# Activation tiles at a wider stride, one chain for keys and values, and shorter norms in an encoder block

## The chip, the core and the metric

The kernel runs on one core of one Trainium2 chip. The time is device microseconds from the start of the program to its end; several executions are taken and their median is given.

## The reference, cut to what matters

One block of an encoder on 256 positions and 2,048 channels, with 256 memory positions, all in float32:

```python
mem_n = rms_norm(mem, mem_norm_g)
h = rms_norm(x, norm_g[0])
q, k, v, g, lr, u_f, u_h, u_s = split(h @ w_in)
y_a = gla_mixer(q, k, v, g, lr, ...)                       # gated linear attention, two directions
y_b = rms_norm(fnet_mixer(u_f), grp_norm_g[0])             # Fourier mixing
y_c = rms_norm(hyena_mixer(u_h, ...), grp_norm_g[1])       # long convolutions
y_d = rms_norm(shortconv_mixer(u_s, sc_conv_w), grp_norm_g[2])
x = x + concatenate([y_a, y_b, y_c, y_d]) @ w_out
x = x + cross_attention(rms_norm(x, norm_g[1]), mem_n, w_xq, w_xkv, w_xo)   # 4 heads of 512
x = x + swiglu(rms_norm(x, norm_g[2]), w_gate_up, w_down)  # 5,632 hidden channels
return rms_norm(x, final_norm_g)
```

`rms_norm(x, g)` is `x * rsqrt(mean(x*x) + 1e-6) * g` over the channels. The group norms `y_b`, `y_c`, `y_d` go over 512 channels each, `y_a` is normed inside its mixer.

## The kernel before

**Tiles.** Activations are kept transposed: 128 channels on the partitions, 256 positions along a partition. A matrix product has to be exact to float32, so each activation tile is `[128, 512]` words: columns 0 to 255 hold the value rounded to the matmul's format (`hi`), 256 to 511 the rest (`lo`). Each 128x128 weight block is likewise split into `wh` and `wl`. One block of a product then takes two matmuls (`mm`, lines 273 and 274): `wh` against all 512 columns, and `wl` against the 256 columns of `hi`. The text calls this a wide block. The two halves of the result are added later by `merge` (line 280, a copy on ScalarE, and an addition on VectorE through the helper at line 178). A narrow block (lines 270, 271, 274) puts all three products in the same 256 columns. 24 tiles `act0` to `act23` lie one behind the other in each partition and serve every stage; the attention adds four `oex` and two `pt` tiles and slots for keys and values, the last stage 36 `f` tiles.

**Weights.** The weights come as one stream `W` in the order of use, in slabs of 128 x 2,048 words (1 MB), issued by SyncE (line 79). A half slab is split by ScalarE (line 89) and VectorE (line 90) ahead of its use. While the list `st.after` has entries, each transfer of a weight piece is followed on the same queue by the next entry; at the start these entries are the loads of the 16 tiles of `mem`.

**Order of the work.** TensorE runs the matrix products in the order `w_xkv`, `w_in`, `w_out`, `w_xq`, `w_xo`, `w_gate_up`, `w_down`. Everything else (mixers, norms, loads of keys and values, softmax) is written as generators in a `Background` queue. After each block, `mm` calls `poll`, which lets a generator take a step when its planned time has come and when VectorE isn't planned to be behind; `drain` runs one generator, or all, to the end. A generator that yields `SOON` (0.01 us) may go on at once, otherwise after 1.3 us (`LAG`). The framework then schedules the instructions for each engine and adds the waits; each engine runs its own queue in order.

**Norms.** `rstd_begin` sums squares over the partitions with matmuls against a column of ones (line 215), one for each half of the positions and for each tile that it is given, and `rstd_cols` takes the inverse root in a few operations on two columns (lines 226 to 237): by an integer first guess and three Newton steps, or, with `root=True` (the final norm alone), by ScalarE's square root, a reciprocal and one step. `rstd_bank` spreads the result over all partitions with two diagonal tiles (line 248) and a matmul (line 250). `group_norm` (lines 499 to 515) squares four tiles on ScalarE and gives all four to `rstd_begin`; three of the four groups are normed by it.

**Keys and values.** `w_xkv` writes keys and values to DRAM in pieces of 128 KB. `load_kv(hd)` brings one head's eight pieces back into tiles `mr` (six buffers, issued by GpSimd, line 576) and splits them (lines 186, 194 and 178); the generators of two heads can be under way together. Before a head's scores are queued, its loads are drained.

**End.** The last `w_down` column is added to the residual, squared and summed; the residual tiles are multiplied by the norm on VectorE (six pairs) and GpSimd (two pairs, line 697), and SyncE stores each pair (256 KB, line 700).

Of the kernel before, what the change touches and what calls it, by code (L numbers as in the profile page):

```python
# [13 lines left out]
F32 = mybir.dt.float32  # L14
# [93 lines left out]
class Background:  # L108
# [32 lines left out]
    def drain(self, g=None):  # L141
        while True:
            q = [e for e in self.q if g is None or e[0] is g]
            if not q:
                break
            for e in q:
                self.step(e)


class Block:  # L150
# [54 lines left out]
    def rstd_begin(self, accs, n, keep=None, root=False):  # L205
# [11 lines left out]
        return self.rstd_cols(p[:, 0:m], n, keep, root)  # L217

    def rstd_cols(self, p, n, keep=None, root=False):
# [7 lines left out]
        if root:  # L227
            nc.scalar.activation(a, v, AF.Sqrt)
            nc.vector.reciprocal(y, a)
# [105 lines left out]
    def run(self):  # L335
        nc, cp = self.nc, self.cp
        st = self.st
        self.act = [cp.tile([P, 512], F32R, name=f"act{i}") for i in range(24)]
# [20 lines left out]
        st.after = [lambda a=a: load("memT", *a) for a in ((1, 1), (2, 1), (3, 1), (4, 1), (5, 1), (6, 2), (8, 2), (10, 2), (12, 2), (14, 2))]  # L359
# [139 lines left out]
    def group_norm(self, y, grp, slots, wait=None):  # L499
# [3 lines left out]
        yield  # L503
        yield
        col = self.rstd_begin([sq], 512)
# [42 lines left out]
    def attention(self):  # L548
        tc, nc, act, st = self.tc, self.nc, self.act, self.st
        with tc.tile_pool(name="atp", bufs=1) as atp, tc.tile_pool(name="kp", bufs=1) as kp, \  # L550
                tc.tile_pool(name="mp", bufs=6) as mp:
# [5 lines left out]
            kv = [None] * 4  # L557
# [11 lines left out]
            def load_kv(hd):  # L569

                kt, vh, vl = [], [], []
                ms = []
                for src in (self.kd, self.vd):
                    for i in range(4 * hd, 4 * hd + 4):
                        ms.append(mp.tile([P, R], F32, name="mr", tag="mr"))
                        nc.gpsimd.dma_start(ms[-1], src[:, i * R:(i + 1) * R])
# [637 lines left out]
```

## Time and profile before

| | us |
|---|---|
| median of 3 runs | 1532.26 |
| lowest to highest | 1532.22 to 1533.97 |
| the profiled execution, its own time | 1531.54 |
| its span in the trace | 1529.7 |
| TensorE busy | 1507.0 |
| TensorE weight loads busy | 1315.1 |
| VectorE busy | 990.7 |
| ScalarE busy | 787.2 |

The span runs from the first to the last recorded instruction, so the profiled execution's own time is 1.8 us longer. Busy times come from the span; weight loads (PEld) overlap the matmuls. The mean granted clock of TensorE was 0.995 of full speed. In the rows that follow, a timeline row gives the start in us, the duration in us, engine, source line, operation, the tiles (output, then inputs) and how many instructions it holds, and in brackets how long the engine had been idle and what ended that. A row of groups gives the count, the busy time in us and the mean in ns. A row of stretches gives the stretch, its length, and for PE and PEld the busy time and the number of instructions, then the granted clock, the DMA engines' busy share and their GB/s. A row of waits gives the total in us, the number of waits and the longest.

### The profile page before, as it was taken

What the parts mean: (1) busy time and instruction counts of PE and PEld (TensorE: products, weight loads), DVE (VectorE), ACT (ScalarE), POOL (GpSimd) and SP (SyncE); (2) the same over time, 40 slices, a digit from 0 to 9 for tenths busy, and PEclk for the clock granted to TensorE, in tenths of its full rate; (3) what the DMA queues carried; (4) which work ended last, traced back from release to release, by engine and by line L of the source; (5) the groups of instructions that cost most, each with busy time, mean ns of one, the idle gap of its engine ahead of it and who ended that gap; (6) DMA issues with size and microseconds to landing.
All of it is one profiled execution on the core that took longest, in us unless ns stands there. A gap on an engine that the chain in (4) does not pass through costs nothing.

```text
span 1529.7 us, 22321 instructions
## 1 busy us (share of the span) xinstructions
PE 1507.0 (99%) x8830; PEld 1315.1 (86%) x8830; DVE 990.7 (65%) x1525; ACT 787.2 (51%) x1238; POOL 39.9 (3%) x76
## 2 busy tenths in 40 slices
PE   8999999999999899999999999999999999999996
PEld 7877788889999788888888888888888888888886
DVE  6676668678656767767766666666666664545553
ACT  6664455547445656656555444444444444444442
POOL 0100100000001100000000000000000000000000
PEclk9999999999999999999999999999999999999998
DMA  9865554354346655444545555555555555555552
GB/s 352 342 237 191 198 190 165 138 190 172 127 167 203 227 187 190 159 151 154 190 169 190 192 193 193 193 189 186 187 186 192 190 192 193 188 179 185 192 193 83
DMA packets 48664, 290.53 MB, mean 190 GB/s; under 512 B 6157, under 2 KB 7470, under 8 KB 16816
## 3 DMA queue, kind: packets, MB, share of 16 engines
q1 hardware_dynamic: 45344, 280.64, 51.7%
q0 software_dynamic: 3072, 8.39, 1.5%
q8 instruction: 69, 1.13, 0.3%
q14 instruction: 35, 0.29, 0.1%
q10 hardware_dynamic: 144, 0.08, 0.0%
HBM read 282.80 MB, written 6.29 MB: 189 GB/s over the span
## 4 chain that ended last, share of the span: by engine, by line
PE 96%; DMA 2%; DVE 1%; ACT 0%; issue 0%; SPq 0%; POOL 0%; DVEq 0%; POOLq 0%; ACTq 0%
PE pg L273 49%; PE pg L274 27%; PE pg L270 3%; PE pg L271 3%; PE pg L325 3%; PE pg L327 2%; PE pg L326 2%; PE pm L273 1%; PE pm L770 1%; DMA mr<-values 1%; PE pm L215 1%; PE pm L620 1%; PE pm L647 0%; PE pm L274 0%; DMA mr<-keys 0%; PE pm L250 0%
## 5 line engine op out<-in xcount | busy, mean ns | idle before, releaser
L273 PE MATMUL pg<-act,wh 128*128 128x512 f32 x2680 | 940.0, 394 | 9.3 <-DVE tmp L178 4.7
L90 DVE TENSOR_TENSOR wl<-raw,wh 128x1024 fp32r<-128x1024 f32 (+1 forms) x507 | 616.9, 1218 | 429.4 <-ACT wh L89 426.0
L274 PE MATMUL pg<-act,wl 128*128 128x256 f32 x3008 | 842.2, 281 | 0.0
L89 ACT CAST wh<-raw 128x1024 fp32r<-128x1024 f32 (+1 forms) x507 | 529.7, 1046 | 592.5 <-PE pg L273 337.4
L273 PEld LDWEIGHTS pg<-act,wh 128*128 128x128 f32 x2680 | 504.5, 188 | 122.7 <-DVE tmp L178 5.1
L274 PEld LDWEIGHTS pg<-act,wl 128*128 128x128 f32 x3008 | 566.9, 189 | 2.6 <-issue 1.6
L273 PE MATMUL pg<-f,wh 128*128 128x512 f32 x540 | 191.3, 399 | 0.0
L274 PE MATMUL pg<-f,wl 128*128 128x256 f32 x576 | 161.8, 281 | 0.0
L273 PEld LDWEIGHTS pg<-f,wh 128*128 128x128 f32 x540 | 101.5, 188 | 25.2
L274 PEld LDWEIGHTS pg<-f,wl 128*128 128x128 f32 x576 | 108.8, 189 | 0.0
L270 PE MATMUL pg<-act,wh 128*128 128x256 f32 x328 | 94.7, 289 | 0.0
L271 PE MATMUL pg<-act,wh 128*128 128x256 f32 x328 | 92.1, 281 | 0.0
L178 DVE TENSOR_TENSOR tmp<-pg,tmp 128x256 f32<-128x256 f32 x183 | 76.1, 417 | 5.0 <-ACT tmp L280 4.0
L280 ACT COPY tmp<-pg 128x256 f32<-128x256 f32 x179 | 64.8, 363 | 14.3 <-PE pg L274 14.3
L325 PE MATMUL pg<-wh,act 128*128 128x512 f32 x160 | 66.4, 415 | 0.0
L327 PE MATMUL pg<-wh,act 128*128 128x512 f32 x160 | 63.3, 396 | 0.0
L326 PE MATMUL pg<-wl,act 128*128 128x512 f32 x160 | 62.9, 393 | 0.0
L270 PEld LDWEIGHTS pg<-act,wh 128*128 128x128 f32 x328 | 61.9, 189 | 0.7
L271 PEld LDWEIGHTS pg<-act,wh 128*128 128x128 f32 x328 | 61.9, 189 | 0.3
L178 DVE TENSOR_TENSOR tmp<-tmp,rs 128x256 f32<-128x256 f32 x88 | 37.3, 425 | 2.9
L325 PEld LDWEIGHTS pg<-wh,act 128*128 128x128 f32 x160 | 30.0, 188 | 10.4 <-issue 2.9
L326 PEld LDWEIGHTS pg<-wl,act 128*128 128x128 f32 x160 | 30.1, 188 | 7.5 <-issue 1.0
(227 smaller groups left out, 985.9 us busy)
## 6 DMA issues: line engine op xcount, KB each, us to landing
raw<-in_W SPq DMA_DIRECT2D x248, 1024.0 KB, 4.8
res<-in_xT SPq DMA_DIRECT2D x8, 512.0 KB, 4.9
raw<-in_W SPq DMA_DIRECT2D x7, 512.0 KB, 7.8
k<-in_mem SPq DMA_DIRECT2D x8, 256.0 KB, 7.7
k<-in_x SPq DMA_DIRECT2D x8, 256.0 KB, 8.3
keys<-tmp POOLq DMA_DIRECT2D x16, 128.0 KB, 5.5
values<-tmp POOLq DMA_DIRECT2D x16, 128.0 KB, 2.3
mr<-keys POOLq DMA_DIRECT2D x16, 128.0 KB, 3.5
```

The costliest lines, as they stand in the source:

```text
L89: nc.scalar.copy(wh[:, a:b], r[:, a:b])
L90: nc.vector.tensor_tensor(out=wl[:, a:b], in0=r[:, a:b], in1=wh[:, a:b].bitcast(F32), op=ALU.subtract)
L178: self.nc.vector.tensor_tensor(out=out, in0=a, in1=b, op=op)
L215: nc.tensor.matmul(p[:, 2 * g + r:2 * g + r + 1], a[:, r * P:(r + 1) * P], self.ones[:, 0:1], start=i == 0, stop=i == len(acc) - 1)
L270: self.nc.tensor.matmul(p[:, 0:R], wh, slot[:, 0:R], start=start, stop=False)
L271: self.nc.tensor.matmul(p[:, 0:R], wh, slot[:, R:512], start=False, stop=False)
L273: self.nc.tensor.matmul(p[:, :], wh, slot[:, :], start=start, stop=False)
L274: self.nc.tensor.matmul(p[:, 0:R], wl, slot[:, 0:R], start=False, stop=stop)
L280: self.nc.scalar.copy(t, p[:, R:512])
L325: nc.tensor.matmul(ps[r][:, :], hi, wh, start=k == 0, stop=False)
L326: nc.tensor.matmul(ps[r][:, :], hi, wl, start=False, stop=False)
L327: nc.tensor.matmul(ps[r][:, :], lo, wh, start=False, stop=k == nk - 1)
```

## The change

Six edits.

- Each `act` tile is 520 words wide, of which the first 512 are used: the tiles lie 2,080 bytes apart in a partition instead of 2,048, and all that is laid out behind them moves by 768 bytes. The buffers `mr` go from six to five.
- The list `st.after` begins with two entries that do nothing, so that the loads of `mem` after the first come two weight pieces later on the queue.
- `group_norm` adds its four squares on VectorE and gives `rstd_begin` the one sum.
- One generator `load_kv` fetches and splits all four heads' keys and values in one chain; a head's scores are a generator that waits for its keys and values, and at the start of the products of heads 2 and 3 the scores of the head two before are drained, other generators being stepped along with it.
- The final norm adds the squares up over the partitions and spreads the sums in one matmul against a full tile of ones, and takes the root on 256 columns. `root` goes out of the helpers.
- The stores alternate between SyncE's queue and ScalarE's.

```diff
--- before.py
+++ after.py
@@ -138,12 +138,12 @@
             if self.owed < OWED and self.now >= e[1]:
                 self.step(e)
 
-    def drain(self, g=None):
+    def drain(self, g=None, others=False):
         while True:
             q = [e for e in self.q if g is None or e[0] is g]
             if not q:
                 break
-            for e in q:
+            for e in list(self.q) if others else q:
                 self.step(e)
 
 
...
@@ -224,15 +224,11 @@
         c = keep.tile([P, 24], F32, name=f"krc{next(self.kept)}") if keep else self.rp.tile([P, 24], F32, name="rc", tag="rc")
         y, v, a = (c[:, 8 * i:8 * i + m] for i in range(3))
         nc.vector.tensor_scalar(out=v, in0=p, scalar1=1.0 / n, scalar2=EPS, op0=ALU.mult, op1=ALU.add)
-        if root:
-            nc.scalar.activation(a, v, AF.Sqrt)
-            nc.vector.reciprocal(y, a)
-        else:
-
-            nc.vector.tensor_scalar(out=a.bitcast(U32), in0=v.bitcast(U32), scalar1=1, scalar2=None, op0=ALU.logical_shift_right)
-            nc.vector.tensor_scalar(out=y.bitcast(I32), in0=a.bitcast(I32), scalar1=-1.0, scalar2=float(0x5f3759df),
-                                    op0=ALU.mult, op1=ALU.add)
-        for _ in range(1 if root else 3):
+
+        nc.vector.tensor_scalar(out=a.bitcast(U32), in0=v.bitcast(U32), scalar1=1, scalar2=None, op0=ALU.logical_shift_right)
+        nc.vector.tensor_scalar(out=y.bitcast(I32), in0=a.bitcast(I32), scalar1=-1.0, scalar2=float(0x5f3759df),
+                                op0=ALU.mult, op1=ALU.add)
+        for _ in range(3):
             self.stt(a, y, -0.5, y, ALU.mult, ALU.mult)
             self.tt(a, a, v, ALU.mult)
             self.stt(y, a, 1.5, y, ALU.add, ALU.mult)
@@ -335,7 +331,7 @@
     def run(self):
         nc, cp = self.nc, self.cp
         st = self.st
-        self.act = [cp.tile([P, 512], F32R, name=f"act{i}") for i in range(24)]
+        self.act = [cp.tile([P, 520], F32R, name=f"act{i}")[:, 0:512] for i in range(24)]
         self.res = [cp.tile([P, 4, R], F32, name=f"res{i}") for i in range(4)]
         self.resk = lambda i: self.res[i // 4][:, i % 4, :]
         self.vec = cp.tile([P, NV], F32, name="vec")
@@ -356,7 +352,8 @@
         nc.vector.memset(warm, 1.0)
         nc.scalar.copy(warm, warm)
         load("memT", 0, 1)
-        st.after = [lambda a=a: load("memT", *a) for a in ((1, 1), (2, 1), (3, 1), (4, 1), (5, 1), (6, 2), (8, 2), (10, 2), (12, 2), (14, 2))]
+        st.after = [lambda: None, lambda: None]
+        st.after += [lambda a=a: load("memT", *a) for a in ((1, 1), (2, 1), (3, 1), (4, 1), (5, 1), (6, 2), (8, 2), (10, 2), (12, 2), (14, 2))]
         nc.vector.memset(self.ones, 1.0)
         make_identity(nc, self.ident)
         with self.tc.tile_pool(name="wx", bufs=1) as st.extra:
@@ -501,8 +498,10 @@
         for j in range(4):
             self.nc.scalar.activation(sq[j], y[:, j, :], AF.Square)
         yield
-        yield
-        col = self.rstd_begin([sq], 512)
+        for j in range(3):
+            self.tt(sq[j + 1], sq[j], sq[j + 1], ALU.add)
+        yield
+        col = self.rstd_begin([sq[3:]], 512)
         yield
         yield
         rs = self.rstd_end(col)
@@ -548,13 +547,13 @@
     def attention(self):
         tc, nc, act, st = self.tc, self.nc, self.act, self.st
         with tc.tile_pool(name="atp", bufs=1) as atp, tc.tile_pool(name="kp", bufs=1) as kp, \
-                tc.tile_pool(name="mp", bufs=6) as mp:
+                tc.tile_pool(name="mp", bufs=5) as mp:
             oex = [atp.tile([P, 512], F32R, name=f"oex{i}") for i in range(4)]
             pt = [atp.tile([P, 512], F32R, name=f"pt{i}") for i in range(2)]
             qs = atp.tile([P, 2], F32, name="qs")
             o = act[0:8] + oex + act[8:12]
             slot = lambda name, n: kp.tile([P, 512], F32R, name=name, tag=name, bufs=n)
-            kv = [None] * 4
+            kv = [([], [], []) for _ in range(4)]
 
             def ev_q(q, p):
                 q.append(slot("q", 8))
@@ -566,39 +565,57 @@
                 nc.vector.tensor_scalar(out=qs, in0=col, scalar1=512 ** -0.5, scalar2=None, op0=ALU.mult)
                 yield
 
-            def load_kv(hd):
-
-                kt, vh, vl = [], [], []
-                ms = []
-                for src in (self.kd, self.vd):
-                    for i in range(4 * hd, 4 * hd + 4):
-                        ms.append(mp.tile([P, R], F32, name="mr", tag="mr"))
-                        nc.gpsimd.dma_start(ms[-1], src[:, i * R:(i + 1) * R])
+            heads = []
+
+            def load_kv():
+
+                todo = [(hd, what, i) for hd in range(4) for what in range(2) for i in range(4)]
+                parts = []
+
+                def fetch():
+                    if len(parts) < len(todo):
+                        hd, what, i = todo[len(parts)]
+                        m = mp.tile([P, R], F32, name="mr", tag="mr")
+                        o = (4 * hd + i) * R
+                        nc.gpsimd.dma_start(m, (self.vd if what else self.kd)[:, o:o + R])
+                        parts.append(m)
+
+                for _ in range(5):
+                    fetch()
+                yield 4
+                for n, (hd, what, i) in enumerate(todo):
+                    while hd > len(heads) + 1:
+                        yield
+                    if what == 0:
+                        kv[hd][0].append(slot("kt", 8))
+                        self.split(kv[hd][0][-1], parts[n])
+                    else:
+                        if i % 2 == 0:
+                            kv[hd][1].append(slot("vh", 4))
+                            kv[hd][2].append(slot("vl", 4))
+                        c = slice(i % 2 * R, i % 2 * R + R)
+                        self.split2(kv[hd][1][-1][:, c], kv[hd][2][-1][:, c], parts[n])
+                    fetch()
+                    yield 1.0
+
+            def scores(hd, q):
+                while len(kv[hd][2]) < 2:
+                    yield
                 yield
-                for m in ms[:4]:
-                    kt.append(slot("kt", 8))
-                    self.split(kt[-1], m)
-                    yield SOON
-                for i, m in enumerate(ms[4:]):
-                    if i % 2 == 0:
-                        vh.append(slot("vh", 4))
-                        vl.append(slot("vl", 4))
-                    c = slice(i % 2 * R, i % 2 * R + R)
-                    self.split2(vh[-1][:, c], vl[-1][:, c], m)
-                    yield SOON
-                kv[hd] = kt, vh, vl
+                yield from self.head(q, *kv[hd], pt, o[4 * hd:4 * hd + 4], qs)
+                heads.append(hd)
 
             lp = [list(range(8)), list(range(8, 16))]
             self.bg.add(scales())
-            loads = [self.bg.add(load_kv(0))]
+            self.bg.add(load_kv())
+            gens = []
             for hd in range(4):
-                if hd < 3:
-                    loads.append(self.bg.add(load_kv(hd + 1)))
                 q = []
+                if hd > 1:
+                    self.bg.drain(gens[hd - 2], True)
                 self.gemm("w_xq", [(4 * hd + i) * P for i in range(4)], self.h2, lambda i, p: ev_q(q, p), first=(4, lp),
                           before=lambda n: n and hd == 0 and self.bg.drain(self.late))
-                self.bg.drain(loads[hd])
-                self.bg.add(self.head(q, *kv[hd], pt, o[4 * hd:4 * hd + 4], qs))
+                gens.append(self.bg.add(scores(hd, q)))
             h3 = self.h3 = act[12:24] + act[0:4]
 
             def ev_o(i, p):
@@ -688,8 +705,17 @@
 
             self.gemm("w_down", [i * P for i in range(16)], f, ev_down,
                       first=(4, [list(range(40)), list(range(40, 44))]), narrow_last=True)
-            p = self.rstd_bank(self.rstd_begin([[self.acc, last]], D, root=True))
-            rs = self.tmp()
+
+            p = self.bank()[:, 0:R]
+            for i, a in enumerate((self.acc, last)):
+                nc.tensor.matmul(p, self.ones, a, start=i == 0, stop=i == 1)
+            v, y, a, rs = (self.tmp() for _ in range(4))
+            nc.vector.tensor_scalar(out=v, in0=p, scalar1=1.0 / D, scalar2=EPS, op0=ALU.mult, op1=ALU.add)
+            nc.scalar.activation(a, v, AF.Sqrt)
+            nc.vector.reciprocal(y, a)
+            self.stt(a, y, -0.5, y, ALU.mult, ALU.mult)
+            self.tt(a, a, v, ALU.mult)
+            self.stt(p, a, 1.5, y, ALU.add, ALU.mult)
             nc.scalar.copy(rs, p)
             for i in range(0, KT, 2):
                 x = self.res[i // 4][:, i % 4:i % 4 + 2, :]
@@ -697,7 +723,7 @@
                     nc.gpsimd.tensor_tensor(out=x, in0=x, in1=rs.unsqueeze(1).to_broadcast([P, 2, R]), op=ALU.mult)
                 else:
                     self.tt(x, x, p.unsqueeze(1).to_broadcast([P, 2, R]), ALU.mult)
-                nc.sync.dma_start(self.t["out"][:, i * R:(i + 2) * R], x.rearrange("p k r -> p (k r)"))
+                (nc.scalar if i % 4 else nc.sync).dma_start(self.t["out"][:, i * R:(i + 2) * R], x.rearrange("p k r -> p (k r)"))
 
 
 class Hyena:
```

More of the change, by code (lines that the diff above doesn't have):

```diff
@@ L203, in sumsq, with rstd_begin @@
             self.tt(acc, acc, s, ALU.add)
-    def rstd_begin(self, accs, n, keep=None, root=False):
+    def rstd_begin(self, accs, n, keep=None):
         nc = self.nc
@@ L216, in rstd_begin, with rstd_cols @@
                                      start=i == 0, stop=i == len(acc) - 1)
-        return self.rstd_cols(p[:, 0:m], n, keep, root)
-    def rstd_cols(self, p, n, keep=None, root=False):
+        return self.rstd_cols(p[:, 0:m], n, keep)
+    def rstd_cols(self, p, n, keep=None):
         nc = self.nc
```

## The prediction

> **What bounds the kernel now.** I read the page first: busy time per engine, the chain that ended last, the costliest groups.
>
> ```profile
> PE 1507.0 (99%) x8830; PEld 1315.1 (86%) x8830; DVE 990.7 (65%) x1525; ACT 787.2 (51%) x1238; POOL 39.9 (3%) x76
> PE 96%; DMA 2%; DVE 1%; ACT 0%; issue 0%; SPq 0%; POOL 0%; DVEq 0%; POOLq 0%; ACTq 0%
> L273 PE MATMUL pg<-act,wh 128*128 128x512 f32 x2680 | 940.0, 394 | 9.3 <-DVE tmp L178 4.7
> L273 PE MATMUL pg<-f,wh 128*128 128x512 f32 x540 | 191.3, 399 | 0.0
> ```
>
> TensorE is busy for 99% of the span and 96% of the chain runs over it. So there are three ways to change the time: fewer matmuls, a different pace of the same matmuls, or the few gaps. The gaps stand in the waits of PE:
>
> ```profile
> PE pg L273 <- DVE tmp L178: 4.7, 1, 4.7
> PE pg L273 <- DVE act L182: 4.6, 1, 4.6
> PE pm L250 <- DVE dg L248: 1.8, 1, 1.8
> PE pm L273 <- ACT wh L89: 1.0, 1, 1.0
> ```
>
> One is the first load, one the last norm (L250), one a wait for weights soon after the start, and one, of 4.7 us, lies in mid-run. For the pace I asked for the busy time of three stretches, each from the start of one "wide block" (a 512-column matmul L273 with its 256-column L274) to the start of another:
>
> ```profile
> 801.75:807.29 5.54, 5.54 (x17) 3.00 (x17) 1.00 0.54 189
> 722.51:728.10 5.59, 5.59 (x17) 3.00 (x17) 1.00 0.54 188
> 1329.63:1345.11 15.48, 15.48 (x46) 8.27 (x45) 1.00 0.57 204
> ```
>
> The first holds 16 blocks on act tiles: 346.5 ns each. The second is a w_xo column, 12 blocks on act tiles and 4 on oex tiles. The third is a w_down group of 8 blocks on act and 36 on f tiles: 44 x 0.3465 would be 15.25.
>
> **Part 1, the stride.** The act tiles' width goes from 512 to 520 words, so tile k moves by 32k bytes. Act tiles sat on multiples of 64 bytes; now every odd one sits 32 bytes past one. oex, pt and f tiles sit 32 bytes past one already, so they show what an "off" tile costs. It isn't nothing: (15.48 - 15.25) / 36 = 6 ns a block in the third stretch, (5.59 - 5.54) / 4 = 12 in the second, where the rounding of the ends leaves 10 to 15 and I use 10. But an off tile in w_down follows other off tiles; after the change each odd tile follows an even one. The starts inside the second stretch, and a stretch where off blocks of the background mix in:
>
> ```profile
> 725.29 0.40 PE L273 MATMUL pg<-oex,wh 128*128 128x512 f32 x1
> 725.98 0.40 PE L273 MATMUL pg<-oex,wh 128*128 128x512 f32 x1
> 726.69 0.40 PE L273 MATMUL pg<-act,wh 128*128 128x512 f32 x1
> 727.40 0.39 PE L273 MATMUL pg<-act,wh 128*128 128x512 f32 x1
> ...
> 693.20 0.40 PE L273 MATMUL pg<-oex,wh 128*128 128x512 f32 x1
> 695.99 0.39 PE L273 MATMUL pg<-act,wh 128*128 128x512 f32 x1
> ```
>
> The first two off blocks after aligned ones take 0.69 together, what two aligned ones take; the next two take 0.71; then two aligned ones 0.71: part of the cost falls on later blocks. From 693.20 to 695.99 lie eight off blocks (4 on oex, 4 of L647 and L648 on pt; the rows between are left out): 0.349 each, 2 ns over. Half of the 2,680 wide blocks are on odd tiles, 1,340. The nearest rows to "one off block behind an aligned one" are the first pair (0 ns) and this mix (2 ns); I take 1.3 ns, **+1.8 us**. Ends: 0, and 10 ns for +13.4; the w_down price, 6, gives +8.0. Below nothing: the pair 725.29 to 725.98 is, by rounding, at best 2 ns a block under an aligned pair; no longer stretch is, so a gain is a rival and not the forecast.
>
> The Trainium skill bears on this: "SBUF — State Buffer", section "Door 1: The DMA port swizzle", has SBUF cachelines of 16 bytes, with a penalty when an access crosses into a new one. 2080 is 130 such lines, so by that rule an odd tile costs no more than an even one and this term would be 0; the f rows above do not agree with it for runs of off tiles, and the measurement decides.
>
> **Part 2, the group squares.** Each of three group norms sums four squares inside its column sums: 2 row halves x 4 tiles.
>
> ```profile
> 333.99 1.84 PE L215 MATMUL pm<-ones,tmp 128*128 128x1 f32 x16
> ...
> 458.11 1.84 PE L215 MATMUL pm<-ones,tmp 128*128 128x1 f32 x16
> ...
> 471.63 0.75 DVE L178 TENSOR_TENSOR act<-res,act 128x256 fp32r<-128x256 f32 x2
> 477.43 0.39 PE L273 MATMUL pg<-act,wh 128*128 128x512 f32 x1
> ```
>
> Sixteen records (two passes of each fp32 matmul) take 1.84; the first and the last of the three norms are shown. After, two matmuls, four records, are left: 12/16 x 1.84 x 3 = 4.1, of which I take **-4.0 us**, as the last record's overhang stays. It comes straight off a TensorE that waits for nothing there. Three adds of some 0.4 us (two of the same size: 0.75 in the fourth row) are put on VectorE, 65% busy, in each norm. Cover: the last norm's final splits end at 471.63 + 0.75 = 472.4 and w_out's first block, which reads them, starts at 477.43; 5 us cover 1.3 us of adds and a matmul or two of delay. Without that cover it would cost 1.3.
>
> **Part 3, the start.** Two weight pieces go to the queue ahead of two mem tiles.
>
> ```profile
> 4.60 1.19 PE L273 MATMUL pg<-act,wh 128*128 128x512 f32 x2 [4.60 <-DVE act L182]
> 8.54 1.21 PE L273 MATMUL pm<-act,wh 128*128 128x512 f32 x4 [1.05 <-ACT wh L89]
> 16.21 0.62 PE L273 MATMUL pg<-act,wh 128*128 128x512 f32 x2
> ```
>
> Between the first and the last row are 24 wide blocks: 11.61 against 24 x 0.3465 = 8.32, so 3.3 are lost, part to a half-rate clock on the first blocks, 1.05 to a named wait for weights. Weights that arrive 256 KB earlier take away most of that wait; mem tile 1 comes later but is needed only eight blocks in. **-0.9**, ends -1.5 (the wait and half of the rest) and +0.5 (a mem tile that comes late).
>
> **Part 4, keys and values.** The mid-run gap:
>
> ```profile
> 499.50 0.28 PE L274 MATMUL pg<-act,wl 128*128 128x256 f32 x1
> 504.52 0.80 PE L273 MATMUL pg<-act,wh 128*128 128x512 f32 x1 [4.74 <-DVE tmp L178]
> 509.81 0.41 PE L273 MATMUL pg<-act,wh 128*128 128x512 f32 x1
> ...
> 500.87 0.40 ACT L186 CAST kt<-mr 128x256 fp32r<-128x256 f32 x1 [3.35 <-DMA mr<-keys]
> 503.09 0.36 ACT L280 COPY tmp<-pg 128x256 f32<-128x256 f32 x1
> 504.05 0.42 DVE L178 TENSOR_TENSOR tmp<-pg,tmp 128x256 f32<-128x256 f32 x1
> ...
> 495.62 8.87 SPq L79 DMA_DIRECT2D raw<-in_W  x2
> 496.22 1.08 POOL L576 DMA_DIRECT2D mr<-keys  x2 [1.53 <-DVE vl L178]
> ...
> mr<-keys POOLq DMA_DIRECT2D x5, 128.0 KB, 2.5
> ```
>
> Two heads' loads go out side by side. ACT stands for 3.35 us at a split whose 128 KB, issued at 496.22, came behind a 1 MB weight slab issued at 495.62 (4.65 us, against a median of 2.5 for five such loads). The merge of the w_out column that PE needs waits behind that split on ACT, then on VectorE, and PE stands 4.74. Then the eight blocks from 504.52 to 509.81 take 5.29 instead of 2.77: another 2.5 at a slow clock. In all 7.4.
>
> After the change one chain loads in the order in which it splits, five buffers deep instead of six. Following it through with these latencies: ACT has 15 of the splits ahead of the same merge copy instead of 13, and loads 13 to 15 are still issued after the slab of 495.62; the copy comes at about 503.0. **-0.4**. Ends: -7.4, if those loads beat the slab (landing 2.5 us after issue, the copy comes near 500.5 and neither gap nor slow clock is left), and +2, if another slab comes between. The same chain moves each head's scores back behind its keys. The list of waits names none of 1 us or more in the attention stretch, so that at most about 1 is to be won from more cover: I take half, **-0.5** (-1 to +1.5). Queued behind the new wait are only background steps; the last head's matmuls are still due before w_xo's second part.
>
> The Trainium skill, "TensorE: Matmul & The Clock Gate", section "What's actually happening", says that after an idle window of about 3.4 us the array runs at half rate until it has been busy about as long; the blocks of 0.64 after the 4.74 gap agree.
>
> **Part 5, tail and stores.**
>
> ```profile
> 1516.84 0.38 PE L215 MATMUL pm<-ones,tmp 128*128 128x1 f32 x2 [0.85 <-ACT tmp L684]
> 1517.70 0.16 DVE L226 TENSOR_SCALAR rc<-pm 128x2 f32<-128x2 f32 x1 [1.37 <-PE pm L215]
> 1518.13 0.17 DVE L229 RECIPROCAL rc<-rc 128x2 f32<-128x2 f32 x1 [0.27 <-ACT rc L228]
> 1519.45 0.70 PE L250 MATMUL pm<-dg,ones 128*128 128x256 f32 x2 [1.79 <-DVE dg L248]
> 1520.19 0.37 ACT L693 COPY tmp<-pm 128x256 f32<-128x256 f32 x1 [2.09 <-PE pm L250]
> 1520.60 3.67 DVE L178 TENSOR_TENSOR res<-res,pm 128x512 f32<-128x512 f32 x6 [1.20 <-ACT tmp L693]
> out_x<-res SPq DMA_DIRECT2D x8, 256.0 KB, 2.8
> ```
>
> Now: sums to 1517.6, a 2-column chain, diagonals, a 256-column matmul, a copy, first multiplication at 1520.60. After: the broadcast matmul comes first, 1516.84 + 0.70 = 1517.54; then six operations over 256 columns at about 0.42 (the 504.05 row) and a copy of 0.37, with hand-overs of about 0.05: near 1520.75. **+0.2**. The reciprocal of 256 columns has no row; from the 0.17 against 0.16 on two columns it may cost up to 5 ns a column: +1.3. Ends -0.8 and +1.8. The second store queue saves issue time only; eight stores of 256 KB that each take 2.8 share the same DMA engines: 0 (-0.3 to +0.3).
>
> **Sum.** The profiled execution took 1531.54, 0.7 under the median of 1532.26. +1.8 - 4.0 - 0.9 - 0.4 - 0.5 + 0.2 = -3.8: 1527.7 for it, **1528.5** for a median. Its own range, with stride from 0 to 2.5 ns and the small terms at their ends: 1526 to 1531.
>
> **Rivals.**
>
> *Off tiles cost their w_xo price (slower).* The rest of the sum is -5.6. At 10 ns for 1,340 odd blocks, +13.4 - 5.6 = +7.8: **1540**. At the w_down price, 6 ns, +2.4: 1534.7, not to be told from before. 0.2% of the time, 3.06 us, is about what a measurement can tell; it is passed from (3.06 + 5.6) / 1340 = 6.5 ns on. For it: the aligned blocks behind off ones at 726.69 are slow too, so a column that alternates may never recover. Against it: the first pair and the mix at 693. Chance 0.32, of which 0.24 lies beyond 6.5 ns.
>
> *The mid-run gap dissolves.* 7.0 more goes: **1521.5**. For it: loads in split order, two fewer transfers in the way. Against it: five buffers and the slab's early issue. Chance 0.18.
>
> *The stride makes blocks shorter.* If the best pair in the rows, 2 ns a block under, became the rule for 2,680 blocks: -5.4 in place of +1.8, **1521**; more if the floor itself gives way. Against it: no stretch in the trace beats 0.3465. Chance 0.08.
>
> The Trainium skill, "TensorE: Matmul & The Clock Gate", section "Wait — 56ns, not 53.3ns?", gives N columns / 2.4 GHz + 2.5 ns between warm matmuls, as an estimate 325 ns for 512 + 256 columns; the rows show 346.5 in fp32r, so by that page there would be something to win, and no row here shows it.
>
> *The chain doesn't do what it says (slower).* With five buffers and each fetch waiting for a split, loads fall behind a second slab: the gap grows from 4.7 to some 10 us. The same sum with +6 instead of -0.4: **1535**. Chance 0.04.
>
> **How the numbers follow.** Forecast 0.38 (faster 0.31, within 0.2% 0.06, slower 0.01), off tiles 0.32 (0.08 within, 0.24 slower), gap gone 0.18 and shorter blocks 0.08 (faster), worse chain 0.04 (slower): faster 0.57, within 0.14, slower 0.29. The range runs from 1515, which leaves out the far half of the shorter blocks, to the 1540 of the w_xo price: about 0.8 of the cases.
>
> **What would show it.** Starts of 16 wide blocks on act tiles 5.55 to 5.58 apart: my stride; 5.62 or more: the first rival; under 5.54: the third. L215 with 4 records per norm, w_out's first block still not waiting. PE's wait for the merge near 500: 4.3 as forecast, under 1 in the second rival. First multiplication of the tail within 0.5 us of 3.9 after the matmul that now stands at 1516.84. I am wrong if the rows of any one of these carry more than 3 us that the sum doesn't have.

## The result, and the profile after

The change makes the kernel slower. Over 20 runs each the median goes from 1532.56 to **1536.27 us** (1533.40 to 1537.24); the ratio is 1.0023, with an interval of 1.0016 to 1.0030: some 3.7 us, where -3.8 were forecast. The profiled execution took 1533.71 (span 1531.7), one of the fastest of the 20.

The page after, its lines of busy time, of the chain, and of the two large groups of TensorE:

```profile
PE 1510.7 (99%) x8788; PEld 1310.5 (86%) x8788; DVE 995.2 (65%) x1532; ACT 787.6 (51%) x1238; POOL 39.9 (3%) x76
PE 98%; DVE 0%; DMA 0%; ACT 0%; SPq 0%; issue 0%; DVEq 0%; ACTq 0%
L269 PE MATMUL pg<-act,wh 128*128 128x512 f32 x2680 | 949.2, 397 | 7.2 <-ACT wh L89 4.6 <-DVE tmp L178 2.6
L269 PE MATMUL pg<-f,wh 128*128 128x512 f32 x540 | 191.5, 399 | 0.0
```

TensorE has 8,788 records instead of 8,830 and yet is busy for 3.7 us more. The group on act tiles (now line 269) went from 940.0 to 949.2 for the same 2,680 matmuls; the group on f tiles stayed. So the pace of the matmuls that touch the moved tiles has changed. Two stretches of the changed kernel show where: 64 wide blocks in mid w_gate_up, all on act tiles, and the w_down group of 8 blocks on act and 36 on f.

```profile
1009.83:1032.28 22.45, 22.45 (x130) 19.55 (x129) 14.36 (x20) 10.72 (x16) 0.00 (x0) 1.00 0.52 188
1330.14:1345.66 15.52, 15.52 (x90) 13.48 (x89) 9.26 (x14) 9.09 (x14) 0.00 (x0) 1.00 0.57 204
```

The columns are as before: stretch, its length, and the busy time of PE, PEld, DVE, ACT and POOL with counts, then clock, DMA share and GB/s. The same 64 blocks of the kernel before:

```profile
1012.52:1034.71 22.19, 22.19 (x131) 19.54 (x129) 14.36 (x20) 10.72 (x16) 0.00 (x0) 1.00 0.53 190
```

PE is busy throughout in both, DVE and ACT do the same work, the clock is full: 0.26 us more for 64 blocks, 4.1 ns a block, or 8.1 for each odd one if the even ones kept their pace. The prediction had 1.3.

The waits of PE after:

```profile
PE pg L269 <- ACT wh L89: 4.6, 1, 4.6
PE pg L269 <- DVE tmp L178: 2.6, 1, 2.6
PE pm L711 <- ACT tmp L701: 0.5, 1, 0.5
```

The mid-run gap is 2.6 instead of 4.7, the one in the last norm is 0.5 instead of 1.8 and 0.8. So the gaps became better while the pace became worse.

### The profile page after: what moved, and what is told of

Same layout as the page of the kernel before. It is cut to its first block, busy times and chain, and to the rows that moved or that the text cites. A ratio compares the mean times of both kernels' runs of the same rounds, so it can differ in the third digit from the quotient of the medians.

```text
span 1531.7 us, 22257 instructions
## 1 busy us (share of the span) xinstructions
PE 1510.7 (99%) x8788; PEld 1310.5 (86%) x8788; DVE 995.2 (65%) x1532; ACT 787.6 (51%) x1238; POOL 39.9 (3%) x76
## 4 chain that ended last, share of the span: by engine, by line
PE 98%; DVE 0%; DMA 0%; ACT 0%; SPq 0%; issue 0%; DVEq 0%; ACTq 0%
PE pg L269 50%; PE pg L270 28%; PE pg L266 3%; PE pg L267 3%; PE pg L321 3%; PE pg L323 2%; PE pg L322 2%; PE pm L269 1%; PE pm L796 1%; PE pm L664 1%; PE pm L270 0%; PE pm L637 0%; DMA raw<-in_W 0%; PE pm L246 0%; PE pm L638 0%; PE pm L665 0%
## 5 line engine op out<-in xcount | busy, mean ns | idle before, releaser
L269 PE MATMUL pg<-act,wh 128*128 128x512 f32 x2680 | 949.2, 397 | 7.2 <-ACT wh L89 4.6
```

What stands on the lines that cost most here:

```text
L269: self.nc.tensor.matmul(p[:, :], wh, slot[:, :], start=start, stop=False)
```

## The experiments

Three questions: is it the stride alone; what about the stride; and what is each other edit worth.

**Stride alone, and all but the stride.** The first is the kernel before with this edit, the second the changed kernel with its first line undone (the buffers `mr` stay five).

```diff
-        self.act = [cp.tile([P, 512], F32R, name=f"act{i}") for i in range(24)]
+        self.act = [cp.tile([P, 520], F32R, name=f"act{i}")[:, 0:512] for i in range(24)]
...
-                tc.tile_pool(name="mp", bufs=6) as mp:
+                tc.tile_pool(name="mp", bufs=5) as mp:
```

> The kernel before with only the act tiles 2,080 bytes apart (and five buffers mr, for room). Theory (alignment): every odd act tile, 32 bytes past a multiple of 64, costs some 8.3 ns a wide block, as the changed kernel's steady columns show (5.61 instead of 5.55 for 16 blocks): 1,372 x 8.3 = +11.4 us, 1544 median, and sixteen blocks near 5.61. Rival (the slowdown comes from the new order of keys, values and scores, not from the addresses): 1532 to 1534, sixteen blocks at 5.55.

Measured: 1541.24 (1540.68 to 1541.93) against 1532.58; ratio 1.0055, 1.0043 to 1.0068. +8.7 us.

> The changed kernel with the act tiles back at 2,048 bytes. Theory: 1536.3 - 11.4 = 1525, the other edits together are worth -7.5 us. Rival (order): 1536, no change from the changed kernel.

Measured: 1527.38 (1526.31 to 1528.20); ratio 0.9964, 0.9951 to 0.9976. That is -5.2 against before and -8.9 against the changed kernel. Both ways the stride costs 8.7 to 8.9 us and the rest gains about 5. The rival of the order falls. The +11.4 expected was too much: it carried the price of w_gate_up into all stages. In the traces of the changed kernel and of the one without the stride the same block begins 0.9 us apart at 775 us, where w_gate_up starts in the second, and 6.7 apart at 1264, where it ends: that stage pays 5.8. The stages ahead of it pay some 3 us, most of which these two traces hide: the changed kernel's start was 0.9 earlier there and its mid-run gap 1.4 shorter.

**Is it alignment to 64 bytes?** The prediction said so. Two kernels in which every act tile starts on a multiple of 64: the changed kernel with a stride of 528 words, and the kernel before with padding that puts weights, f, oex and pt on such multiples too.

```diff
-        self.act = [cp.tile([P, 520], F32R, name=f"act{i}")[:, 0:512] for i in range(24)]
+        self.act = [cp.tile([P, 528], F32R, name=f"act{i}")[:, 0:512] for i in range(24)]
```

> The changed kernel with the act tiles 2,112 bytes apart, so that all of them start on multiples of 64 bytes but are no longer back to back. Alignment: as at 2,048 bytes, 1525, sixteen blocks at 5.55. Rival (what costs is that the tiles lie apart, or any stride that is no power of two): 1536 or more, sixteen blocks at 5.61.

Measured: 1534.86 (1532.46 to 1535.29); ratio 1.0013, 1.0004 to 1.0022. The two stretches:

```profile
1013.26:1035.77 22.51, 22.51 (x130) 19.53 (x129) 14.37 (x20) 10.72 (x16) 0.00 (x0) 1.00 0.54 187
1333.31:1348.62 15.31, 15.31 (x90) 13.45 (x89) 9.29 (x14) 9.12 (x14) 0.00 (x0) 1.00 0.57 207
```

All tiles aligned, and the act blocks are no faster than with 2,080 bytes (351.7 ns a block against 350.8). The f blocks, which still lie 32 bytes off, are nearly at the floor: 15.31 instead of 15.48.

```diff
-        self.vec = cp.tile([P, NV], F32, name="vec")
+        self.vec = cp.tile([P, NV + 8], F32, name="vec")[:, 0:NV]
...
-            qs = atp.tile([P, 2], F32, name="qs")
+            qs = atp.tile([P, 16], F32, name="qs")[:, 0:2]
```

> The kernel before with 32 bytes of padding behind vec (and as much behind qs), so that weights, f, oex and pt also start on multiples of 64 bytes. Alignment: 540 f blocks lose 6 ns, 64 oex blocks 10 ns, the 480 matmuls with a weight tile as the moving operand some 4 ns: -3.2 -0.6 -1.9 = -5.7 us, 1527. Rival (f and oex blocks are slow for where they lie or for what runs beside them): 1532.5, w_down groups unchanged at 15.48.

Measured: 1543.30 (1540.94 to 1543.54); ratio 1.0063, 1.0050 to 1.0076. Here nothing was done to the act tiles or their stride; the weights, and all else behind `vec`, moved by 32 bytes:

```profile
1018.11:1040.58 22.47, 22.47 (x130) 19.69 (x129) 14.36 (x20) 10.72 (x16) 0.00 (x0) 1.00 0.54 187
1338.62:1354.14 15.52, 15.52 (x90) 13.48 (x89) 9.26 (x14) 9.09 (x14) 0.00 (x0) 1.00 0.56 204
```

The act blocks became slow (351.1 ns) and the f blocks, now aligned, stayed slow. Both kernels speak against alignment, and the second says that the place of something behind `vec` counts. That gave a new theory: what counts is the distance between the moving tile and the weight tile in a partition. All weight blocks start at the same place modulo 256 bytes, since a block is 512 bytes long. In what follows the distance is the weight tile's start less the act tile's, modulo 256: 96 in the kernel before, 128 in the padded one; f tiles have 0 in all of these. With a stride of 2,080 the 24 act tiles run through all eight multiples of 32.

**One distance for all tiles.** Unused bytes in front of the act tiles and behind `vec` move act against all the rest; the stride is 2,048. In the first kernel everything moves together.

```diff
+        cp.tile([P, 8], F32, name="pad")
         self.act = [cp.tile([P, 512], F32R, name=f"act{i}") for i in range(24)]
```

> The kernel before with 32 unused bytes in front of the act tiles, so that everything lies 32 bytes higher: act, weights, f and oex keep their distances, but act now lies 32 bytes past multiples of 64. Theory (distance): what counts is where the moving tile lies against the weight tile, modulo 256 bytes; distances are those of before, so a wide act block stays at 346.7 ns, f stays at 353, time about 1532. Rival (alignment of the moving tile to 64 bytes): act blocks at about 353, time near 1549; f blocks at 346.7.

Measured: 1532.77, one execution. The two stretches:

```profile
1013.68:1035.86 22.18, 22.18 (x130) 19.52 (x129) 14.36 (x20) 10.71 (x16) 0.00 (x0) 1.00 0.55 190
1330.78:1346.26 15.48, 15.48 (x90) 13.47 (x89) 9.25 (x14) 9.09 (x14) 0.00 (x0) 1.00 0.57 204
```

Every act tile lies 32 bytes past a multiple of 64, and every block is as fast as before; f is aligned and slow. Alignment has fallen from both sides. In the next runs, one execution each, act moves by 32, 64, ... bytes, with `res` and `vec` behind it, and all that lies behind `vec` by 512; the edit for 128:

```diff
+        cp.tile([P, 32], F32, name="pad")
         self.act = [cp.tile([P, 512], F32R, name=f"act{i}") for i in range(24)]
...
-        self.vec = cp.tile([P, NV], F32, name="vec")
+        self.vec = cp.tile([P, NV + 96], F32, name="vec")[:, 0:NV]
```

> The kernel before with 32 bytes in front of act and 480 behind vec: act moves by 32 bytes, all else by 512, so act lies 32 bytes nearer to the weights modulo 256. Distance: slow, 350 to 359 ns a block (the odd tiles with this distance show 359 in the changed kernel), time 1542 or more. Alignment: also slow, about 353. Rival (only tiles of mixed addresses are slow): 346.7.

Measured: 1541.51.

```profile
1016.75:1039.37 22.62, 22.62 (x131) 19.64 (x130) 14.36 (x20) 10.73 (x16) 0.00 (x0) 1.00 0.52 186
1338.95:1354.49 15.54, 15.54 (x91) 13.50 (x90) 9.27 (x14) 9.09 (x14) 0.00 (x0) 1.00 0.55 203
```

> As the run before with act moved by 64 bytes, all else by 512. Distance: not the distance of before, so 347 to 350 ns (such tiles in the changed kernel: 346.7, at the wider stride of 2,112: 350), 1532 to 1542. Alignment: 346.7 and 1532.

Measured: 1540.56.

```profile
1018.79:1041.40 22.61, 22.61 (x130) 19.63 (x129) 14.36 (x20) 10.72 (x16) 0.00 (x0) 1.00 0.53 186
1340.08:1355.39 15.31, 15.31 (x91) 13.46 (x89) 9.29 (x14) 9.12 (x14) 0.00 (x0) 1.00 0.58 207
```

> Act moved by 96 bytes, all else by 512: distance 0 modulo 256, that of the f tiles. By the odd tiles of the changed kernel with this distance 349.8 ns a block; by the f blocks 347 or 353. Rival (only multiples of 64 matter): as act_by_32, 353.

Measured: 1531.09.

```profile
1014.91:1037.09 22.18, 22.18 (x130) 19.38 (x129) 14.35 (x20) 10.72 (x16) 0.00 (x0) 1.00 0.53 190
1331.07:1346.32 15.25, 15.25 (x91) 13.33 (x89) 9.29 (x14) 9.09 (x14) 0.00 (x0) 1.00 0.59 207
```

> As the run before with act moved by 128 bytes, all else by 512. Distance: 350 to 353 ns (such tiles in the changed kernel: 351, at 2,112: 353), time 1543 to 1551. Alignment: 346.7 and 1532.

Measured: 1527.68.

```profile
1011.69:1033.87 22.18, 22.18 (x130) 19.66 (x129) 14.36 (x20) 10.72 (x16) 0.00 (x0) 1.00 0.55 190
1327.89:1343.16 15.27, 15.27 (x90) 13.47 (x89) 9.29 (x14) 9.11 (x14) 0.00 (x0) 1.00 0.58 207
```

> Act moved by 160 bytes, all else by 512. By the tiles of the changed kernel with this distance 350.6 ns a block. Rival (multiples of 64 matter): as act_by_32, 353.

Measured: 1545.76.

```profile
1020.93:1043.55 22.62, 22.62 (x131) 19.73 (x129) 14.35 (x20) 10.71 (x16) 0.00 (x0) 1.00 0.53 186
1342.72:1358.26 15.54, 15.54 (x91) 13.49 (x90) 9.26 (x14) 9.10 (x14) 0.00 (x0) 1.00 0.56 203
```

> Act moved by 192 bytes, all else by 512. By the tiles of the changed kernel with this distance 354 ns a block, at the stride of 2,112 also 354: time 1543 or more. Rival (multiples of 128 and 64 are good): 346.7.

Measured: 1540.75.

```profile
1021.03:1043.43 22.40, 22.40 (x130) 19.54 (x129) 14.35 (x20) 10.72 (x16) 0.00 (x0) 1.00 0.54 188
1339.92:1355.26 15.34, 15.34 (x91) 13.48 (x90) 9.29 (x14) 9.12 (x14) 0.00 (x0) 1.00 0.58 206
```

> The kernel before with act moved by 256 bytes and all else by 512. Theory (distance modulo 256): as in the kernel before, act blocks at 346.7 ns and f blocks at 353, about 1532. Rival (a longer period, or other address bits): another pace, 350 to 353 ns and 1542 or more.

Measured: 1530.89.

```profile
1011.76:1033.95 22.19, 22.19 (x131) 19.54 (x129) 14.36 (x20) 10.71 (x16) 0.00 (x0) 1.00 0.52 190
1328.87:1344.35 15.48, 15.48 (x91) 13.47 (x89) 9.25 (x14) 9.09 (x14) 0.00 (x0) 1.00 0.56 204
```

The first length of each pair divided by 64 is the pace on act tiles in mid w_gate_up:

| act moved by | distance | ns a block on act | w_down group, us |
|---|---|---|---|
| 0 (before) and 256 | 96 | 346.7 | 15.48 |
| 32 | 64 | 353.4 | 15.54 |
| 64 | 32 | 353.3 | 15.31 |
| 96 | 0 | 346.6 | 15.25 |
| 128 | 224 | 346.6 | 15.27 |
| 160 | 192 | 353.4 | 15.54 |
| 192 | 160 | 350.0 | 15.34 |
| 224 (the weights moved by 32) | 128 | 351.1 | 15.52 |

What follows: in w_gate_up the pace on act tiles goes with the distance, is the same again after 256 bytes, and has three good values of eight. The kernel before stood on one of them; the stride of 2,080 bytes sends the tiles through all eight, that of 2,112 through four. The expectations drawn from single tiles of the changed kernel failed in size: its tiles with distance 32 showed 346.7 ns and those with 64 showed 359, where both cost 353 when all tiles have them. In a mixed column the cost of one block shows up at a neighbour, and the table doesn't add up either: its mean over the eight distances is 350.1 ns against 350.8 measured at 2,080 bytes, over the four 349.2 against 351.7 at 2,112. It ranks layouts in which all tiles have one distance and doesn't price a mixed one.

The f blocks tell the second thing. Their own distance is 0 in all eight of these moves, and the group takes either 15.25 to 15.34 or 15.48 to 15.54, whichever way act was moved. So the distance of a tile alone doesn't set its pace. With distance 0 throughout (act moved by 96) act in w_gate_up and f are both at the floor; behind act blocks of another distance the same f blocks can stay slow for all 36. That fits a pattern that is set by what ran ahead and then kept. The trace with act moved by 96 shows it for act tiles. The first row is a stretch of 64 blocks in w_xo, all on act and oex tiles at distance 0; then come starts of blocks on act tiles around a background matmul of a norm (L250), with the rows between left out:

```profile
736.12:758.73 22.61, 22.61 (x130) 19.60 (x129) 15.76 (x24) 12.34 (x21) 0.00 (x0) 1.00 0.52 185
...
787.32 0.39 PE L273 MATMUL pg<-act,wh 128*128 128x512 f32 x1
791.21 0.40 PE L273 MATMUL pg<-act,wh 128*128 128x512 f32 x1
791.57 0.59 PE L250 MATMUL pm<-dg,ones 128*128 128x256 f32 x2
792.35 0.40 PE L273 MATMUL pg<-act,wh 128*128 128x512 f32 x1
796.16 0.39 PE L273 MATMUL pg<-act,wh 128*128 128x512 f32 x1
```

In w_xo these blocks take 353.3 ns. The eleven blocks from 787.32 to 791.21 take 3.89 us, 353.6 each; the eleven from 792.35 to 796.16, at the same distance, take 3.81, 346.4 each, and 346.6 is the pace still in mid w_gate_up. So at distance 0 there are two paces, and a short interruption led from one to the other, once, in one execution. In w_xo 64 such blocks took 22.35 us in the kernel before and 22.24 with act moved by 128: the distances 96 and 224 were good in this stage too.

Two things are argued and not shown. The weights were never moved without all else behind `vec`, so that the weight tile is the partner is the likeliest reading and no more. And what collides stays open. VectorE and ScalarE are unlikely: with act moved by 32, the blocks of w_gate_up during which VectorE is busy throughout and those during which it is idle take 353.3 ns alike, and so it is for ScalarE.

**The other edits, one at a time,** each as the kernel before with that part of the diff alone.

```diff
-        yield
-        col = self.rstd_begin([sq], 512)
+        for j in range(3):
+            self.tt(sq[j + 1], sq[j], sq[j + 1], ALU.add)
+        yield
+        col = self.rstd_begin([sq[3:]], 512)
```

> The kernel before with only the three additions of the group squares on VectorE. Theory (TensorE records come off one for one): 36 records less, -4.1 us, as between 306 and 466 us in the run without the stride, so 1528.4. Rival (the additions delay the last norm and w_out waits): -2.7 or less gain, with a wait of PE near 474.

Measured: 1528.46 (1527.41 to 1529.34) against 1532.96; ratio 0.9971, 0.9960 to 0.9983: -4.5 us. The trace adds that the mid-run gap is 4.0 here instead of 4.7, though keys and values are loaded as before. That gap spreads: with act moved by 256 and by 128, where nothing but the layout differs from the kernel before, it is 3.0 and 4.8.

```diff
-            loads = [self.bg.add(load_kv(0))]
+            self.bg.add(load_kv())
...
-                self.bg.add(self.head(q, *kv[hd], pt, o[4 * hd:4 * hd + 4], qs))
+                gens.append(self.bg.add(scores(hd, q)))
```

> The kernel before with only the single chain for keys and values (five buffers). Theory: the mid-run gap shrinks from 4.74 to about 4.0 and fewer blocks run at the slow clock, -1.6, and the attention stretch gives another -0.5: 1530.4. Rival (the chain helps only because the group norms moved the weights' transfers): the gap stays at 4.7 or grows, 1532.5 or more.

Measured: 1532.04 (1530.42 to 1533.49); ratio 0.9996, 0.9987 to 1.0004: -0.9, not told apart from no change. The gap is 4.2, its stretch (488 to 518 us) 0.7 shorter, the attention 0.5. The size lies between theory and rival.

```diff
-            p = self.rstd_bank(self.rstd_begin([[self.acc, last]], D, root=True))
...
+            for i, a in enumerate((self.acc, last)):
+                nc.tensor.matmul(p, self.ones, a, start=i == 0, stop=i == 1)
...
-                nc.sync.dma_start(self.t["out"][:, i * R:(i + 2) * R], x.rearrange("p k r -> p (k r)"))
+                (nc.scalar if i % 4 else nc.sync).dma_start(self.t["out"][:, i * R:(i + 2) * R], x.rearrange("p k r -> p (k r)"))
```

> The kernel before with only the new end: the norm on 256 columns and the two store queues. Theory (the reciprocal of 256 columns takes 1.75 us, not 0.42): +1.4 to the first multiplication, -0.4 behind it, +1.0, so 1533.5. Rival (the stores hide it): 0, 1532.5. Both are near what five rounds can tell; the trace decides by its first multiplication, 4.7 us after the residual's last addition in the kernel before and 6.1 here.

Measured: 1533.48 (1532.12 to 1534.81); ratio 1.0007, 0.9998 to 1.0015. The timing can't tell it from zero. The trace can; the last residual addition and two operations behind it:

```profile
1518.22 0.42 DVE L178 TENSOR_TENSOR res<-res,pg 128x256 f32<-128x256 f32 x1 [6.45 <-PE pg L274]
1520.79 1.75 DVE L698 RECIPROCAL tmp<-tmp 128x256 f32<-128x256 f32 x1 [0.48 <-ACT tmp L697]
1524.36 1.88 DVE L178 TENSOR_TENSOR res<-res,pm 128x512 f32<-128x512 f32 x3 [0.44 <-ACT tmp L702]
```

From the addition to the first multiplication it is 6.14 us, against 4.7 before; from there to the end of the span 1533.0 - 1524.36 = 8.64, against 1529.7 - 1520.60 = 9.10. So +1.45 - 0.46 = +1.0.

**The parts that gain, on the good distance.** No stride, act moved by 128, the end of the kernel before but with two store queues.

```diff
-        self.act = [cp.tile([P, 520], F32R, name=f"act{i}")[:, 0:512] for i in range(24)]
+        cp.tile([P, 32], F32, name="pad")
+        self.act = [cp.tile([P, 512], F32R, name=f"act{i}") for i in range(24)]
...
+        self.vec = cp.tile([P, NV + 96], F32, name="vec")[:, 0:NV]
...
+            p = self.rstd_bank(self.rstd_begin([[self.acc, last]], D, root=True))
```

> The changed kernel with the act tiles back at 2,048 bytes and moved by 128 bytes against the weights, and the end of the kernel before with two store queues. Theory: 1527.4 without the stride, -5 for f, oex and pt blocks at 346.7 as in the run with act moved by 128, -1.4 for the reciprocal: 1521. Rival (f blocks at the floor were a matter of luck in that one execution): 1526, f blocks at 353.

Measured: **1520.78** (1519.52 to 1521.49) against 1532.96; ratio 0.9922, 0.9908 to 0.9935: 12 us under the kernel before, 15 under the changed one.

```profile
1004.14:1026.32 22.18, 22.18 (x130) 19.66 (x129) 14.37 (x20) 10.72 (x16) 0.00 (x0) 1.00 0.55 190
1320.34:1335.61 15.27, 15.27 (x91) 13.46 (x89) 9.29 (x14) 9.12 (x14) 0.00 (x0) 1.00 0.58 207
```

The f blocks are fast again, as in the one execution with act moved by 128, and all five executions lie within 2 us: no luck.

## Why the prediction was wrong, step by step

The sum said -3.8; +3.7 was measured. That lies inside the stated range, but on the side of the first rival, which had a chance of 0.32, between its two times of 1534.7 and 1540. The kernel without the stride has the same pace as before, so that the start of one and the same block in both shows what the other edits gained up to it. Rows of the kernel before, then of the one without the stride:

```profile
306.58 0.40 PE L325 MATMUL pg<-wh,act 128*128 128x512 f32 x1
465.59 0.28 PE L270 MATMUL pg<-act,wh 128*128 128x256 f32 x1
518.15 0.39 PE L273 MATMUL pg<-act,wh 128*128 128x512 f32 x1
722.51 0.39 PE L273 MATMUL pg<-act,wh 128*128 128x512 f32 x1
1515.36 0.28 PE L270 MATMUL pg<-f,wh 128*128 128x256 f32 x1
```

```profile
306.56 0.40 PE L321 MATMUL pg<-wh,act 128*128 128x512 f32 x1
461.51 0.28 PE L266 MATMUL pg<-act,wh 128*128 128x256 f32 x1
512.40 0.39 PE L269 MATMUL pg<-act,wh 128*128 128x512 f32 x1
716.21 0.39 PE L269 MATMUL pg<-act,wh 128*128 128x512 f32 x1
1509.06 0.28 PE L266 MATMUL pg<-f,wh 128*128 128x256 f32 x1
```

The lead is 0.02, 4.08, 5.75, 6.30 and 6.30 us.

- **The stride: +1.8 forecast, +8.7 to +8.9 measured.** This step failed, in its mechanism and in its size. I had read the slow f and oex blocks as the price of lying 32 bytes off a multiple of 64; they were the only tiles with another address, but they also had another distance to the weights, and I didn't separate the two. Then, between rows of 0, 2, 6 and 10 ns, I took those with the fewest blocks in a row as nearest to an alternating column. The rows at 726.69 and 727.40, where aligned blocks paid behind off ones, already said that a short sequence doesn't show its own cost. The first rival, with 10 ns and its point of decision at 6.5 for an odd tile, had the size: 8.1 in w_gate_up, 6.6 if the whole 8.8 us is spread over its 1,340 odd blocks. Its reason was as wrong as mine. What the runs showed in place of both: the pace goes with the distance between an act tile and what lies behind `vec`, and the stride sends act tiles that all stood at a good distance through all eight. The prediction's own sign stood between the two: sixteen act blocks took 22.45 / 4 = 5.61, over the 5.55 to 5.58 of the forecast and just under the rival's 5.62.
- **The rule of 16-byte lines.** The kernels with act moved by 32 and by 64 bytes, both multiples of 16, cost 353 ns against 346.7. The Trainium skill, "SBUF — State Buffer", section "Door 1: The DMA port swizzle", has a penalty for crossing into a new 16-byte line; by that rule alone they would cost nothing, and these runs do not agree.
- **The squares: -4.0 forecast, -4.06 measured** between 306 and 466 us. Right, with its cover: L215 has 12 records left for the three norms, and the list of PE's waits names none at w_out's first block.
- **The start: -0.9 forecast, 0.0 in this pair, some -1.4 as an estimate over more traces.** At 306.58 the two kernels are level, but that execution of the kernel before had started early. The start spreads, so here is the same block in the kernel before, in the one with the new end alone, whose start is the old one, and in the last kernel, whose start is the new one:

```profile
306.58 0.40 PE L325 MATMUL pg<-wh,act 128*128 128x512 f32 x1
308.65 0.40 PE L325 MATMUL pg<-wh,act 128*128 128x512 f32 x1
306.38 0.40 PE L325 MATMUL pg<-wh,act 128*128 128x512 f32 x1
```

 In the seven traces that have the old start and the pace of the kernel before up to there, the block begins between 306.58 and 308.65, at 307.9 on average; in the two with the new start, at 306.38 and 306.56. So the term was probably right in its sign, and -1.4 lies near the early end, -1.5, of its range; two traces with the new start are few. In the changed kernel the later wait for weights, 1.0 in the kernel before, is gone from the list of waits.
- **Keys and values: -0.4 and -0.5 forecast, -1.7 and -0.55 in this pair** from 466 to 518 and to 722 us. The second is right: the chain alone gives 0.5 there and the squares alone nothing. The first is not the chain's: the stretch around the gap is as much shorter, 1.7 us, with the squares alone, whose loads are those of before. The gap is 4.1 on average, 3.0 to 4.8, in the twelve traces with the old loads and 3.8 on average, 2.6 to 4.2, in the five with the chain, so that -0.4 may be right and one execution of each can't settle it. Why it spreads stays open; that it hangs on when the pieces meet a weight slab is not shown. The prediction's sign for it, a wait of 4.3, came out at 2.6 in the changed kernel; the rivals in which it dissolves (under 1) or grows (some 10) did not happen. The 7.4 us that the prediction gives the gap count from the start at which the waiting block was due; the two numbers beside it, 4.74 and 2.5, make 7.2.
- **The end: +0.2 forecast, +1.0 measured.** I costed the 256-column reciprocal as any other operation, 0.42. It is 1.75:

```profile
1517.85 0.70 PE L711 MATMUL pm<-tmp,ones 128*128 128x256 f32 x2 [0.53 <-ACT tmp L701]
1519.04 0.42 ACT L714 ACTIVATE tmp<-tmp 128x256 f32<-128x256 f32 x1 [0.70 <-DVE tmp L713]
1519.49 1.75 DVE L715 RECIPROCAL tmp<-tmp 128x256 f32<-128x256 f32 x1 [0.48 <-ACT tmp L714]
1523.07 3.67 DVE L178 TENSOR_TENSOR res<-res,pm 128x512 f32<-128x512 f32 x6 [0.44 <-ACT tmp L719]
```

 The bound of 5 ns a column, from 0.17 against 0.16 on two columns, was the right end: 0.42 + 1.3 = 1.72. The Trainium skill, "VectorE: DVE Perf Modes", section "First, the fixed hardware budget", says that a reciprocal runs as a repeated divide with a repeat count of 8 on the pipe; the row agrees with a repeated operation, at 4 times the plain one. The stores gained 0.46 where I gave 0: in the trace of the new end alone the first store is issued 0.72 us behind the start of the first multiplication, in the kernel before 1.34. The prediction's sign for the end, 3.9 us from the last matmul to the first multiplication within 0.5, came out at 1523.07 - 1517.85 = 5.2.

Without the stride my terms are -5.6, and that kernel measured -5.2. With the stride at 8.8 the sum would have been +3.2, against +3.7 measured: 7.0 of the 7.5 us of error are the stride. The other terms nearly hold in their sum; that the missed reciprocal doesn't show in it is luck.

## What to carry to other kernels

When two classes of tiles run at different paces, list every way in which their addresses differ before giving the pace to one of them, and price a change of layout by a run, not by the nearest rows: here a shift of 32 bytes of the *weights*, with all else behind `vec`, cost some 10 us, more than the stride itself. In a kernel that TensorE bounds, try a few offsets of the activations against the weights; the best took 512 unused bytes in a partition, 128 in front of the act tiles and 384 behind `vec`, and the one execution of it was 5 us faster. Compare more than one trace before giving a microsecond to an edit at the start or in a gap: here such stretches spread by 2 us between kernels that are the same there. Cost an operation on 256 columns by a row of that operation, since two columns hide its rate.

## What the runs showed of the hardware that I had not expected

- A matmul pair of 512 and 256 columns takes between 346.6 and 353.4 ns at the same granted clock, by the place of its moving tile against the weights and all that moved with them, with the same value after 256 bytes.
- The pace of a run of blocks with one distance can be either of two values (15.25 to 15.34, or 15.48 to 15.54 us for the group with 36 f blocks; 353.6 or 346.4 ns for act blocks at distance 0 within one execution), and it was kept until something changed it: there, one interruption by a background matmul.
- An fp32 reciprocal on VectorE takes 1.75 us for 256 columns, where an addition takes 0.42.
